# Bias and row maximum of the attention scores in one DVE operation

## The chip, the cores and the metric

The kernel runs on one core of a Trainium2 chip. The metric is the time of one execution on the device in microseconds (us), as the median of several runs. A profiled execution also gives a trace: every instruction of every engine with its start and its duration. The engines are PE (TensorE, matrix products), DVE (VectorE, elementwise work and reductions along a row), ACT (ScalarE, activation functions), POOL (GpSimd) and SP (the queue that issues the transfers). Each runs its own instructions in order and waits on semaphores for the others.

## What is computed

Two layers of a hybrid decoder over 256 tokens of width 1024. In each layer an attention group of 8 heads and a state-space group of 16 heads read the same normalised input through one input projection, and an output projection adds the result to the stream. This is the part of the reference that the change touches, cut to what matters for 256 tokens (where a query sees only the one block of its own):

```python
q = rms_norm(q.reshape(b, s, 8, 128), q_norm_w)
k = rms_norm(k.reshape(b, s, 8, 128), k_norm_w)
slopes = exp2(-8.0 * h / 8)                    # h = 1..8
s_own = einsum('hqd,hcd->hqc', q, k) * dh ** -0.5
s_own = s_own - slopes * (t_query - t_key)
s_own = where(t_query >= t_key, s_own, -inf)
p = softmax(s_own, axis=-1)
attn = einsum('hqc,hcd->hqd', p, v) * silu(g)
```

## The kernel before

Activations lie with 128 partitions; tokens come in two tiles of 128. Every projection is computed as three products of a split form (fp32r): the weights are split into a high part `wh` (an ACT cast, line 101) and a low part `wl` (a DVE subtraction, line 102), the input into `hT` and `lT`, and PE adds high x high, low x high and high x low (lines 226 to 228 with tokens on the partitions, lines 244 to 246 with channels on them). The weights, about 77 MB, stream in by DMA into four `raw` buffers; up to eight split pieces are held ahead of PE.

The projections go through in the order v, q and k of heads 0 to 3, q and k of heads 4 to 7, x (the state-space input, tiles `xb`), g, z, and the output. The small products of attention and of the state-space part are laid between them: each is a generator that yields a number of ticks and goes on that many weight pieces later. A scheduler then orders the instructions of every engine by its own estimate of when their inputs are there, so that the written order is a priority and not the final order. It stands ahead of the run: the engines follow the order that it fixed.

`qk_post` normalises q and k. ACT squares and sums a tile of 4 heads (`ss`), DVE computes `se` (line 344, 128x4: for q it is `ss + 128 eps`, so that the factor 128^-0.5 of the scores is in it), POOL raises it to the power -0.5 (`rr`, line 185), DVE multiplies (`qn`, line 348), PE transposes (`qtp`, line 354), and ACT writes `qT` or `kT`.

`attn_head` does one head. PE computes the scores `sp` of both query tiles in PSUM (line 362: the first 128 queries against 128 keys; line 363: the second 128 against 256), so a row of 384 holds 128 and then 256 scores. DVE adds the bias (line 365): `base` holds the distance and the causal mask without the slope, and one operation over 384 columns multiplies it by the slope and adds the scores. Two reductions give the negated maxima `mx` (lines 367 and 368). ACT takes the exponential with `mx` as bias and sums it (lines 370 and 371). DVE takes the reciprocal and scales both parts (lines 374 to 376). PE then transposes the probabilities (`pp`, line 380), ACT copies them (`pT`, line 382), and PE multiplies by v (`po`, lines 386 and 387). There are 8 heads a layer, 16 in all.

## Time and profile before

| | |
|---|---|
| time, median of 3 runs | 453.02 us (452.85 to 453.19) |
| the profiled execution: its time | 452.3 us |
| the profiled execution: its span | 450.5 us |
| PE busy | 446.1 us, 99% of the span |
| weight loads of PE (PEld) | 406.0 us, 90% |
| DVE busy | 346.7 us, 77% |
| ACT busy | 279.7 us, 62% |
| POOL busy | 23.9 us, 5% |
| granted clock of PE | full in all slices |

The span runs from the first to the last instruction that the profile shows; some 1.8 us of the execution's time lie around it. Busy times of one engine do not add to those of another: they overlap. A matmul's duration in the trace is longer than the step from its start to the next one's start, since matmuls are pipelined, so PE's steps are read from the starts.

### The profile page before, as it was taken

To read this page: it belongs to the slowest core of one execution; us is meant where nothing else is said; L and a number is where in the kernel's file an instruction comes from. 1 tells how busy PE (TensorE), PEld (TensorE's weight loads), DVE (VectorE), ACT (ScalarE), POOL (GpSimd) and SP (SyncE) were. 2 spreads that over 40 slices of the span, in tenths; PEclk is the share of its full clock that TensorE was granted. 3 is DMA by queue.
4 is the path that set the end of the run, shared out by engine and by line. 5 is a ranking of instruction groups with operands and counts; after the bars stand their busy time and mean duration, and the time that the engine had idled before them with its cause. 6 is when DMAs were issued, how large, how long until landed. Compare 5 with 4: busy or idle time off the path is not lost.

```text
span 450.5 us, 7880 instructions
## 1 busy us (share of the span) xinstructions
PE 446.1 (99%) x2956; PEld 406.0 (90%) x2956; DVE 346.7 (77%) x636; ACT 279.7 (62%) x571; POOL 23.9 (5%) x29
## 2 busy tenths in 40 slices
PE   9999999999999999999999999999999999999997
PEld 9998878999999999888899878889999989998986
DVE  7597876799999888766565784686999999787621
ACT  7776779778558645534556656977657865555400
POOL 0000320200000000000000011110000000000000
PEclk9999999999999999999999999999999999999999
DMA  8888886452355155556246988561435444553301
GB/s 282 275 250 294 284 302 249 143 185 95 95 188 176 60 160 186 169 188 182 61 138 232 284 278 288 185 227 53 139 109 175 139 141 128 200 180 121 121 25 70
DMA packets 26373, 79.43 MB, mean 176 GB/s; under 512 B 2624, under 2 KB 9440, under 8 KB 25824
## 3 DMA queue, kind: packets, MB, share of 16 engines
q1 hardware_dynamic: 26048, 78.68, 53.3%
q8 instruction: 23, 0.38, 0.3%
q10 hardware_dynamic: 288, 0.27, 0.2%
q14 instruction: 14, 0.11, 0.1%
HBM read 77.85 MB, written 1.08 MB: 175 GB/s over the span
## 4 chain that ended last, share of the span: by engine, by line
PE 99%; DVE 0%; issue 0%
PE o L227 6%; PE o L226 6%; PE o L228 6%; PE xb L244 5%; PE xb L246 5%; PE xb L245 5%; PE z L245 3%; PE v L228 3%; PE z L244 3%; PE v L226 3%; PE v L227 3%; PE z L246 3%; PE k L227 3%; PE g L246 3%; PE g L244 3%; PE g L245 3%
## 5 line engine op out<-in xcount | busy, mean ns | idle before, releaser
L102 DVE TENSOR_TENSOR wl<-raw,wh 128x1024 fp32r<-128x1024 f32 (+3 forms) x145 | 166.0, 1157 | 41.3 <-ACT wh L101 40.1
L101 ACT CAST wh<-raw 128x1024 fp32r<-128x1024 f32 (+3 forms) x145 | 143.9, 999 | 59.8 <-DMA raw<-in_w_dram 15.9
L244 PE MATMUL xb<-hT,wh 128*128 128x256 f32 x192 | 56.3, 293 | 0.0
L245 PE MATMUL xb<-lT,wh 128*128 128x256 f32 x192 | 54.4, 283 | 0.0
L246 PE MATMUL xb<-hT,wl 128*128 128x256 f32 x192 | 53.9, 281 | 0.0
L245 PEld LDWEIGHTS xb<-lT,wh 128*128 128x128 f32 x192 | 36.2, 189 | 0.3
L246 PEld LDWEIGHTS xb<-hT,wl 128*128 128x128 f32 x192 | 36.2, 189 | 0.1
L244 PEld LDWEIGHTS xb<-hT,wh 128*128 128x128 f32 x192 | 36.2, 188 | 0.2
L246 PE MATMUL g<-hT,wl 128*128 128x256 f32 x128 | 36.3, 283 | 0.0
L245 PE MATMUL z<-lT,wh 128*128 128x256 f32 x128 | 36.2, 283 | 0.0
L244 PE MATMUL g<-hT,wh 128*128 128x256 f32 x128 | 36.1, 282 | 0.0
L244 PE MATMUL z<-hT,wh 128*128 128x256 f32 x128 | 36.0, 281 | 0.0
L245 PE MATMUL g<-lT,wh 128*128 128x256 f32 x128 | 35.9, 281 | 0.0
L246 PE MATMUL z<-hT,wl 128*128 128x256 f32 x128 | 35.9, 280 | 0.0
L447 DVE SCALAR_TENSOR_TENSOR cv<-rw,par_sb,cv 128x256 f32<-128x256 f32 x72 | 31.6, 481 | 4.2 <-ACT cv L444 4.2
L226 PE MATMUL k<-wh,hT 128*128 128x512 f32 x64 | 25.4, 397 | 0.0
L227 PE MATMUL k<-wh,lT 128*128 128x512 f32 x64 | 25.4, 397 | 0.0
L228 PE MATMUL k<-wl,hT 128*128 128x512 f32 x64 | 25.4, 397 | 0.0
L227 PE MATMUL q<-wh,lT 128*128 128x512 f32 x64 | 25.1, 394 | 0.0
L226 PE MATMUL q<-wh,hT 128*128 128x512 f32 x64 | 25.1, 394 | 0.0
L227 PE MATMUL o<-wh,al 128*128 128x512 f32 (+1 forms) x64 | 24.7, 386 | 0.0
L228 PE MATMUL q<-wl,hT 128*128 128x512 f32 x64 | 24.6, 395 | 0.0
(197 smaller groups left out, 1106.6 us busy)
## 6 DMA issues: line engine op xcount, KB each, us to landing
raw<-in_w_dram SPq DMA_DIRECT2D x120, 512.0 KB, 4.3
raw<-in_w_dram SPq DMA_DIRECT2D x15, 348.0 KB, 3.7
cb<-cd SPq DMA_DIRECT2D x4, 1024.0 KB, 7.8
raw<-in_w_dram SPq DMA_DIRECT2D x8, 344.0 KB, 3.6
x<-in_x_dram SPq DMA_DIRECT2D x2, 512.0 KB, 5.2
xT<-in_w_dram SPq DMA_DIRECT2D x3, 256.0 KB, 4.3
out_dram<-x SPq DMA_DIRECT2D x3, 256.0 KB, 2.0
raw<-in_w_dram SPq DMA_DIRECT2D x2, 174.0 KB, 3.2
```

The source lines that it names most:

```text
L101: nc.scalar.copy(h[:, ks, :wd], src[:, ks, :wd])
L102: nc.vector.tensor_tensor(lo[:, ks, :wd], src[:, ks, :wd], h[:, ks, :wd].bitcast(F32), ALU.subtract)
L226: pe.matmul(ps[:, cs], lh[:, kl, tl], wh[:, kk, cs], start=first, stop=False)
L227: pe.matmul(ps[:, cs], ll[:, kl, tl], wh[:, kk, cs], start=False, stop=False)
L228: pe.matmul(ps[:, cs], lh[:, kl, tl], wl[:, kk, cs], start=False, stop=final)
L244: pe.matmul(o, wh[:, kk, cs], lh[:, k, :], start=(k == 0 and c == 0), stop=False)
L245: pe.matmul(o, wh[:, kk, cs], ll[:, k, :], start=False, stop=False)
L246: pe.matmul(o, wl[:, kk, cs], lh[:, k, :], start=False, stop=(k == KT - 1 and c == 1))
L447: dve.scalar_tensor_tensor(cv[:, c, :], rw[:, c, k:k + S], cw(k), cv[:, c, :], ALU.mult, ALU.add)
```

## The change

For each head the multiplication of `base` by the slope is taken out of the DVE operation. Scores and bias are held divided by the slope: q carries the factor 1/slope, put in through `slope2` (the squared slope of every head, 8 memsets on POOL at the start) in the small operation `se` of q; the exponential multiplies by the slope again through its scale. With no factor left, bias and maximum are one DVE operation (`tensor_tensor_reduce`: add, then maximum along the row), once for the 128 and once for the 256 columns. A small operation of 128x2 multiplies both maxima by minus the slope.

```diff
+    slope2 = const.tile([P, NH], F32, name="slope2")
+    for h in range(NH):
+        pool.memset(slope2[:, h:h + 1], 4.0 ** -(h + 1))
@@ qk_post
-        dve.tensor_scalar(se, ss, a, b, ALU.mult, ALU.add)
+        if col == C_QN:
+            dve.scalar_tensor_tensor(se, ss, b, slope2[:, 4 * c:4 * c + 4], ALU.add, ALU.mult)
+        else:
+            dve.tensor_scalar(se, ss, a, b, ALU.mult, ALU.add)
@@ attn_head
-        dve.scalar_tensor_tensor(sc, base, 2.0 ** -(h + 1), sp[:, 0:384], ALU.mult, ALU.add)
+        mp = small.tile([P, 2], F32, tag="mp", name="mp")
+        for i, cs in enumerate((slice(0, 128), slice(128, 384))):
+            dve.tensor_tensor_reduce(sc[:, cs], base[:, cs], sp[:, cs], 1.0, -3.0e38,
+                                     ALU.add, ALU.max, mp[:, i:i + 1])
         mx = small.tile([P, 2], F32, tag="mx", name="mx")
-        dve.tensor_reduce(mx[:, 0:1], sc[:, 0:128], AX.X, ALU.max, negate=True)
-        dve.tensor_reduce(mx[:, 1:2], sc[:, 128:384], AX.X, ALU.max, negate=True)
+        slope = 2.0 ** -(h + 1)
+        dve.tensor_scalar(mx, mp, -slope, None, ALU.mult)
-        act.activation(sc[:, 0:128], sc[:, 0:128], AF.Exp, bias=mx[:, 0:1], accum_out=sm[:, 0:1])
+        act.activation(sc[:, 0:128], sc[:, 0:128], AF.Exp, bias=mx[:, 0:1], scale=slope,
+                       accum_out=sm[:, 0:1])
```

(and the same scale in the second exponential). In the built program each of the two new operations is a pair: the operation over the row, and one of 128x1 that writes the maximum. The scheduler orders all engines anew. On DVE, at the first head of the first layer, this stands in a row before (`se` belongs to k of heads 4 to 7, `wl` is a weight piece's low part):

```order
L365 SCALAR_TENSOR_TENSOR sc<-base,sp 128x384
L344 TENSOR_SCALAR se<-ss 128x4
L102 TENSOR_TENSOR wl_973<-raw_877,wh_972 128x1024
L367 TENSOR_REDUCE mx<-sc 128x1
L368 TENSOR_REDUCE mx<-sc 128x1
L344 TENSOR_SCALAR se<-ss 128x4
```

and this now:

```order
L374 ISA sc,mp<-base,sp 128x128
L374 ISA mp 128x1
L374 ISA sc,mp<-base,sp 128x256
L374 ISA mp 128x1
L350 TENSOR_SCALAR se<-ss 128x4
L102 TENSOR_TENSOR wl_983<-raw_887,wh_982 128x1024
L378 TENSOR_SCALAR mx<-mp 128x2
L350 TENSOR_SCALAR se<-ss 128x4
```

The weight piece stands between the scores and the maximum in both; three operations of the head have become five. On PE, where that first head's probabilities are transposed (`pp`) in the stream of the x projection, this stood in a row:

```order
L244 MATMUL xb_1072<-hT_135,wh_754 128x256
L245 MATMUL xb_1072<-lT_136,wh_754 128x256
L246 MATMUL xb_1072<-hT_135,wl_755 128x256
L244 MATMUL xb_1072<-hT_135,wh_754 128x256
L245 MATMUL xb_1072<-lT_136,wh_754 128x256
L246 MATMUL xb_1072<-hT_135,wl_755 128x256
L244 MATMUL xb_1072<-hT_135,wh_772 128x256
L245 MATMUL xb_1072<-lT_136,wh_772 128x256
L380 MATMUL pp<-ident,sc 128x128
L354 MATMUL qtp<-ident,qn 128x128
L380 MATMUL pp<-ident,sc 128x128 x2
L354 MATMUL qtp<-ident,qn 128x128 x7
```

and this stands there now, from the same matmul on:

```order
L247 MATMUL xb_1083<-hT_144,wh_763 128x256
L391 MATMUL pp<-ident,sc 128x128
L360 MATMUL qtp<-ident,qn 128x128
L391 MATMUL pp<-ident,sc 128x128 x2
L360 MATMUL qtp<-ident,qn 128x128 x7
L248 MATMUL xb_1083<-lT_145,wh_763 128x256
L249 MATMUL xb_1083<-hT_144,wl_764 128x256
```

The transposes stand seven matmuls of the x projection earlier. PE's instructions are the same 2611 rows in both programs, in another order at such places; the runs of plain fp32 products that interrupt the split ones are 71 before and 76 now. The order on SP is unchanged, and up to the first head DVE's differs only in the kind of the `se` of q.

## Rows read from the trace of the kernel before

**Rows 1.** The page: span, busy time of each engine, slices of DVE and PE's clock.
```profile
span 450.5 us, 7880 instructions
...
PE 446.1 (99%) x2956; PEld 406.0 (90%) x2956; DVE 346.7 (77%) x636; ACT 279.7 (62%) x571; POOL 23.9 (5%) x29
...
DVE  7597876799999888766565784686999999787621
...
PEclk9999999999999999999999999999999999999999
```
**Rows 2.** The page's chain that ended last, shares of the span by engine.
```profile
PE 99%; DVE 0%; issue 0%
```
**Rows 3.** Waits of PE, all of them: who waited for whom, us, times, longest.
```profile
PE warm L165 <- DVE ones L159: 1.1, 1, 1.1
```
**Rows 4.** Timeline of PE: start us, us, line, operation, tiles; an alone-standing score product.
```profile
80.55 0.38 PE L362 MATMUL sp<-kT,qT 128*128 128x128 f32 x2
80.77 0.60 PE L363 MATMUL sp<-kT,qT 128*128 128x256 f32 x2
81.02 0.47 PE L244 MATMUL xb<-hT,wh 128*128 128x256 f32 x1
81.32 0.28 PE L245 MATMUL xb<-lT,wh 128*128 128x256 f32 x1
81.44 0.28 PE L246 MATMUL xb<-hT,wl 128*128 128x256 f32 x1
```
**Rows 5.** Timeline of PE: first head's transposes (pp) and what follows without a break.
```profile
86.89 0.27 PE L380 MATMUL pp<-ident,sc 128*128 128x128 f32 x1
87.00 0.27 PE L354 MATMUL qtp<-ident,qn 128*128 128x128 f32 x1
87.11 0.38 PE L380 MATMUL pp<-ident,sc 128*128 128x128 f32 x2
87.33 0.93 PE L354 MATMUL qtp<-ident,qn 128*128 128x128 f32 x7
88.09 0.39 PE L362 MATMUL sp<-kT,qT 128*128 128x128 f32 x2
88.32 0.60 PE L363 MATMUL sp<-kT,qT 128*128 128x256 f32 x2
88.56 0.47 PE L246 MATMUL xb<-hT,wl 128*128 128x256 f32 x1
88.87 0.28 PE L244 MATMUL xb<-hT,wh 128*128 128x256 f32 x1
```
**Rows 6.** Timeline of DVE: the first head's probabilities are scaled, last part.
```profile
84.03 0.35 DVE L376 TENSOR_SCALAR sc<-sc,ri 128x256 f32<-128x256 f32 x1
```
**Rows 7.** Groups by line: out<-in, shapes, xcount | busy us, mean ns | idle before.
```profile
L365 DVE SCALAR_TENSOR_TENSOR sc<-base,sp 128x384 f32<-128x384 f32 x16 | 8.8, 551 | 1.6 <-PE sp L363 0.9 <-PE pp L380 0.5
...
L368 DVE TENSOR_REDUCE mx<-sc 128x1 f32<-128x256 f32 x16 | 6.6, 411 | 0.0
...
L367 DVE TENSOR_REDUCE mx<-sc 128x1 f32<-128x128 f32 x16 | 4.5, 282 | 0.1
...
L370 ACT ACTIVATION_READ_ACCUMULATOR sc<-sc,mx 128x1 f32 x16 | 3.2, 200 | 0.0
...
L344 DVE TENSOR_SCALAR se<-ss 128x4 f32<-128x4 f32 x16 | 2.6, 162 | 0.0
...
L458 DVE SCALAR_TENSOR_TENSOR cm<-bp,tri 128x256 f32<-128x256 f32 x4 | 1.7, 414 | 0.0
...
L460 DVE SCALAR_TENSOR_TENSOR cm<-bp,tri 128x128 f32<-128x128 f32 x4 | 1.1, 282 | 0.0
...
L526 DVE TENSOR_SCALAR nv<-np 128x2 f32<-128x2 f32 x4 | 0.6, 151 | 0.0
```
**Rows 8.** Timeline of POOL: its work at the start.
```profile
0.83 0.56 POOL L169 IOTA io<- 128x512 f32 x1 [0.39 <-POOLq L754]
16.68 0.56 POOL L185 TENSOR_TENSOR rs<-me,mhalf 128x1 f32<-128x1 f32 x1 [15.28 <-DVE me L308]
```

## The prediction

> **What bounds the kernel now.** I read the page's busy times first: of a span of 450.5 us PE is busy for 446.1, DVE for 346.7, ACT for 279.7 [rows 1]. That alone does not settle it, since matmuls overlap in the trace. The second view is the chain that ended last, followed back from the last instruction: 99% of it is PE, and DVE has 0% [rows 2]. The third is the list of PE's waits, and it holds one line: 1.1 us ahead of the warm-up matmuls at the very start [rows 3]. So no score, mask or probability keeps PE waiting long enough to be listed. The fourth is the timeline of PE, for which the starts count: two split matmuls of 256 columns stand 0.12 us apart (81.32 and 81.44), and the next product starts at that pace whatever it belongs to [rows 4]. [...] The kernel is a stream of matmuls that PE takes one after the other, and its time is the sum of their steps.

> DVE matters only where it is late for PE. It is 90% busy or more in slices 9 to 13 and 29 to 34 [rows 1], some 90 to 146 and 315 to 383 us, and the heads lie in and just ahead of these stretches. There the question is how much time passes between the end of DVE's work for a head and PE's use of it. For the first head the last scaling of the probabilities ends at 84.03 + 0.35 = 84.38 [rows 6], and the two transposes that need it start at 87.11 [rows 5]: a margin of 2.7 us.

> **The change part by part, DVE.** A head loses one operation of 551 ns and two reductions of 411 and 282: 1244 ns [rows 7]. It gains two combined operations, two writes of the maximum and one of 128x2. The trace has no combined operation. Its nearest rows are the two-input operations that also read PSUM: 282 ns for 128 columns and 414 for 256 [rows 7], 696 together; that is the lower end, as the maximum comes on top of it. The upper end is that the row is passed twice, once to add and once to reduce: 282 + 282 and 414 + 411, 1389 together [rows 7]. I take the lower, because the new instruction reads the same two inputs and writes the same output as those rows. The write of the maximum has no row on DVE; the nearest is ACT's read of its accumulator, 200 ns, and on the low side it could hide wholly behind the next operation, 0; the smallest DVE operation shown, of 128x2, takes 151 [rows 7], and I take that for it and for the product with the slope. The sum is 696 + 3 x 151 = 1149 ns, 0.1 us less a head, 1.5 us over 16 heads. The ends are 696 + 0 + 151 = 847 and 1389 + 400 + 151 = 1940, so 0.4 us less to 0.7 us more a head.

> [...]

> None of this is on the path that sets the end: what covers it is PE's own stream, and DVE's 1.5 us stay as idle time of DVE. If the cover went (PE waiting for a head), each us that a head comes late would count in full.

> **The small edits.** The `se` of q becomes an operation of the same size with one more input, 162 ns before [rows 7], eight times; anything up to twice that, 0.16 us, lies ahead of a POOL operation and a transpose, and only the q tiles wait for it. I put it at nothing, with 0.2 us for the range. The scale in the exponential is an operand of an operation that is there already: nothing. The eight memsets of `slope2` stand on POOL behind the iota, which ends at 0.83 + 0.56 = 1.39 us, and POOL's next work begins at 16.68 [rows 8]; at the iota's 0.56 us each, the dearest row, they would take 4.5 us of the 15 that are idle there. Nothing. The first exponential of a head now waits for both maxima instead of its own: 0.41 us later than before at most [rows 7], out of the margin.

> **PE's order.** PE's instructions are the same, so its sum of steps can change only through neighbours. The runs of plain fp32 products among the split ones go from 71 to 76, which looks like five more interruptions. Their price is read from two places. The score products alone, from 80.55 to the second split matmul after them at 81.32, less one step of 0.12, cost 0.65 us [rows 4]. Behind eleven transposes the same products, from 88.09 to 88.87 less 0.12, cost 0.66 [rows 5]. Breaking a run up costs 0.01 us, so five breaks cost nothing that can be seen; I allow 0.3 us either way.

> The order also spends margin. The first head's transposes stand seven split matmuls earlier, 7 x 0.12 = 0.8 us, so they come at 87.11 - 0.8 = 86.3, and 1.9 of the 2.7 us are left. Against that stand 0.1 us gained on DVE (0.7 lost at the upper end) and 0.4 for the later first exponential. It remains positive at both ends: 1.6 and 0.8 us.

> **The sum.** Against the profiled execution, 450.5 of span and 1.8 around it: PE's steps 0 (within 0.3), DVE 0 on the path, `se` 0 to 0.2, start 0. That gives 452.3 for an execution like the profiled one. The three runs have their median at 453.02, 0.7 higher, so the forecast for the median is 453.0.

> **Rivals.** *Slower: the combined operation is much dearer than its parts, and PE waits for the heads.* The point from which this decides is a head that ends more than the 1.9 us later than before; or a lasting excess, since where DVE is full [rows 1] a head's excess is handed to the next. At the upper end of 0.7 us a head, 8 heads a layer would gather 5.6 us if DVE had no idle time at all between them; less 1.9 of margin that is 3.7 a layer, 7.4 for both, 460.4. With half of the excess caught by DVE's idle time it is 2.8 - 1.9 = 0.9 a layer, 454.8. For it: no row shows the operation, and DVE is full in those slices. Against it: the excess needs the upper end of every bound at once. I give it 0.09.

> *Faster: PE has room that its busy time hides, and DVE's saving comes out.* Then up to 16 x 0.4 = 6.4 us at the lower end of DVE's cost, or 1.5 at my value, would show: 446.6 or 451.5. For it is that PE's busy time counts overlapping matmuls, and that weight loads fill only 406.0 us [rows 1]. Against it are the chain, the single wait, and starts that follow each other at a constant step [rows 2 to 5]: nothing there waits for DVE. I give it 0.04. [...]

> *The change does not do what it says:* if the combined operation passes the row twice, DVE does not become faster at all. That alone leaves the time at 453.0, since only the slow rival's excess is felt; it is in the first case.

> **How the numbers follow.** What a measurement of this kernel can tell from no change is about 0.2%, 0.9 us. The forecast, no change, has 0.87; the slow rival 0.09; the fast one 0.04. These are also the chances of same, slower and faster. For the range I take the spread of the runs and PE's 0.3 below, which gives 452.4, and above the 0.3 of PE, 0.2 of `se`, the spread, and some tenths of waiting, 454.1. That leaves out most of both rivals, less than 2 in 10.

> **What would show it.** In the profile of the changed kernel PE's list of waits should again hold the warm-up alone, the chain should stay at 99% PE, and the span should lie within half a us of 450.5. DVE's busy time should fall by 1 to 3 us; the combined rows should take about 282 and 414 ns. The forecast is wrong if a transpose of probabilities or a score product appears among PE's waits, if the weight pieces on DVE come late in slices 9 to 13 or 29 to 34, or if PE's steps at the 76 interruptions turn out longer than the same contents before.

## The result and the profile after

The changed kernel takes 456.69 us (median of 4 runs, 456.24 to 457.53); the kernel before, timed beside it, takes 452.94 (452.70 to 453.19). The ratio is 1.0084, with a 95% interval of 1.0063 to 1.0104. The forecast was 453.0 and no change: it was 3.7 us too low, and 456.69 lies above its range of 452.4 to 454.1. The kernel before ran again beside every experiment below, and one of those runs, at 1574.94 us, is left out of all ratios.

The profiled execution of after took 457.53 us, the highest of the four, with a span of 455.6; before it was 450.5 [rows 1]. So 5.1 us of span are to be found. First the page of after: span, busy times, PE's clock in 40 slices, and the chain that ended last.

```profile
span 455.6 us, 7918 instructions
...
PE 450.7 (99%) x2956; PEld 407.2 (89%) x2956; DVE 342.3 (75%) x668; ACT 280.7 (62%) x571; POOL 27.2 (6%) x37
...
PEclk9999999999999999999999999999999999999999
...
PE 85%; DMA 6%; DVE 3%; ACT 3%; issue 2%; POOL 0%; SPq 0%; ACTq 0%; POOLq 0%
```

DVE's busy time fell by 4.4 us, from 346.7. PE's rose by 4.6, from 446.1, with the same 2956 instructions and the clock granted in full in every slice, as in [rows 1]. The second view is PE's list of waits (us in total, times, longest).

```profile
PE warm L165 <- DVE ones L159: 1.1, 1, 1.1
PE pp L391 <- DVE sc L386: 0.4, 1, 0.4
PE v L231 <- DVE wl L102: 0.2, 1, 0.2
```

Two waits are new against [rows 3], 0.6 us together. They don't make 5.1, though the chain seems to say more, with PE at 85% where [rows 2] had 99%. Its list in order of time shows why: at PE's wait for the scaled probabilities (`sc`), at 88.28 us, the chain, followed back, leaves PE, and it has no piece of PE's from there down to 22.5 us. Three of its pieces (start, us, what):

```profile
31.10 4.40 DMA raw<-in_w_dram
...
66.27 10.44 DMA raw<-in_w_dram
...
85.92 0.69 DVE qn L354
```

In all that time PE was working. A wait of 0.4 us is enough for the other path to be the one that ended last; the shares don't say what it cost. The rest has to lie between PE's instructions, so the third view is PE's timeline, read by its starts. Here are two ends of the same stretch of the k projection, 20 steps of 512 columns apart with nothing between them. Before:

```profile
41.34 0.39 PE L226 MATMUL k<-wh,hT 128*128 128x512 f32 x1
...
45.91 0.39 PE L228 MATMUL k<-wl,hT 128*128 128x512 f32 x1
```

After:

```profile
42.26 0.39 PE L229 MATMUL k<-wh,hT 128*128 128x512 f32 x1
...
46.92 0.39 PE L231 MATMUL k<-wl,hT 128*128 128x512 f32 x1
```

That is 4.57 / 20 = 0.2285 us a step before and 4.66 / 20 = 0.233 after. **Each matmul starts later behind the last one, though nothing waits and the clock is full.** The durations (0.39) don't show it; only the starts do. In the x projection, where a step has 256 columns, 26 steps lie between these rows of before:

```profile
82.01 0.28 PE L245 MATMUL xb<-lT,wh 128*128 128x256 f32 x1
...
84.96 0.28 PE L244 MATMUL xb<-hT,wh 128*128 128x256 f32 x1
```

and between these of after:

```profile
82.93 0.28 PE L249 MATMUL xb<-hT,wl 128*128 128x256 f32 x1
...
86.00 0.28 PE L248 MATMUL xb<-lT,wh 128*128 128x256 f32 x1
```

2.95 / 26 = 0.1135 before, 3.07 / 26 = 0.118 after. The slow pace is not new in itself. In the z projection the kernel before has it too: 32 steps of its timeline, from 161.38 to 165.15, take 0.118 each.

```profile
161.38 0.28 PE L246 MATMUL z<-hT,wl 128*128 128x256 f32 x1
...
165.15 0.28 PE L245 MATMUL z<-lT,wh 128*128 128x256 f32 x1
```

So before has two paces, in 512 columns as well: 20 steps of q, from 250.82 to 255.49, take 0.2335 each. After has the quick one of 256 columns in places (10 steps of x, from 321.56 to 322.69, take 0.113 each) and the slow one more of the time. Of neighbouring split matmuls of 256 columns, some 490 pairs start 0.11 us apart in before's timeline and some 355 in after's; of 512 columns, some 95 pairs start 0.22 apart in before's and none in after's. To put one number on it, I took from each trace all pairs of neighbouring split matmuls of the same width with nothing between them (about 680 pairs of 512 columns, 1330 of 256) and the mean distance of their starts: 229.9 and 116.4 ns before, 233.3 and 117.4 after. The program has 720 matmuls of 512 and 1440 of 256: 720 x 3.4 = 2.5 us and 1440 x 1.0 = 1.4, together **3.9 of the 5.1 us**. The first head's wait gives 0.4. Some 0.6 pass at the very start: the v projection's matmul behind the second new wait starts at 25.83, its counterpart before at 25.25. That leaves 0.2; the 288 matmuls of 344 and 348 columns in the v projections are not in this count.

The medians differ by 3.75 us, less than the spans of the two profiled executions. The pace alone is enough for that.

### The profile page after: what moved, and what is told of

The parts are those of the page before. It is cut to its first block, busy times and chain, and to the rows that moved or that the text cites. A ratio compares the mean times of both kernels' runs of the same rounds, so it can differ in the third digit from the quotient of the medians.

```text
span 455.6 us, 7918 instructions
## 1 busy us (share of the span) xinstructions
PE 450.7 (99%) x2956; PEld 407.2 (89%) x2956; DVE 342.3 (75%) x668; ACT 280.7 (62%) x571; POOL 27.2 (6%) x37
## 4 chain that ended last, share of the span: by engine, by line
PE 85%; DMA 6%; DVE 3%; ACT 3%; issue 2%; POOL 0%; SPq 0%; ACTq 0%; POOLq 0%
PE o L229 6%; PE o L231 6%; PE o L230 6%; DMA raw<-in_w_dram 5%; PE xb L249 4%; PE xb L248 4%; PE xb L247 4%; PE g L247 3%; PE z L248 3%; PE g L249 3%; PE z L247 3%; PE g L248 3%; PE z L249 3%; PE v L231 3%; PE v L229 3%; PE v L230 3%
## 5 line engine op out<-in xcount | busy, mean ns | idle before, releaser
L188 POOL TENSOR_TENSOR rr<-se,mhalf 128x4 f32<-128x4 f32 x16 | 19.1, 1192 | 121.3 <-DVE se L348 82.3
L229 PE MATMUL o<-wh,ah 128*128 128x512 f32 (+1 forms) x64 | 24.7, 386 | 0.0
```

Source lines behind the costliest of these rows:

```text
L188: pool.tensor_tensor(o, i, mhalf[:, :n], ALU.pow)
L229: pe.matmul(ps[:, cs], lh[:, kl, tl], wh[:, kk, cs], start=first, stop=False)
```

## The experiments

What could change the step of an unchanged matmul? The change adds two tiles to SBUF. `slope2`, 32 bytes per partition, stands in the first pool, ahead of all operands of the projections. `mp`, four buffers of 32 bytes, stands in the pool of small tiles, which lies between the activations (`hT`, `lT`) and the weight buffers (`raw`, `wh`, `wl`). In the built program the first `hT` lies at byte 38016 of a partition before and 38048 after, the first `wh` at 162752 and 162912. All activations have moved by 32 bytes, all weights by 160, and the distance between the two operands of a split matmul has grown by 128. The theories were: operands have to lie at multiples of 64 bytes; the address of one operand decides; the distance between the two decides; the heads' new work costs the time after all. In every kernel below the order of PE's, ACT's and DVE's instructions is that of its parent; a kernel made from before has one or two memsets more on POOL.

**Alignment.** After, with `slope2` twice as large, so that all operands are at multiples of 64 again.

```diff
-    slope2 = const.tile([P, NH], F32, name="slope2")
+    slope2 = const.tile([P, 2 * NH], F32, name="slope2")
```

> The changed kernel with slope2 made 64 instead of 32 bytes wide per partition (half of it unused), so that every tile behind it starts 32 bytes later and on a multiple of 64 again; the order of every engine is that of the changed kernel. Theory A (the addresses: the 32 bytes of slope2 shift the matmul operands and the DMA targets off multiples of 64, and PE's steps become longer: 512 columns 233 instead of 229 ns, 256 columns 118 instead of 114): the slow steps become as rare as in the kernel before, time 452.5 to 453.9. Theory B (the combined operation and the new order make PE wait): nothing changes, 456.2 to 457.5. Theory C (the price of 4 us is spread over both): 454 to 455.5.

Measured: 457.17 us, 1.0093 of before (1.0078 to 1.0108), steps of 233.3 and 117.6 ns. Nothing came back. The distance is still 128 larger: alignment to 64 is not the cause. The time is also what was expected if the combined operation and the new order made PE wait; that theory falls with the whole change at the old distance, below.

**Moving all, the activations, or the weights of the kernel before.** Three kernels without any part of the change. The first puts an unused tile of 32 bytes into the first pool (everything moves by 32), the second one there and one in the small pool (activations by 32, weights by 64), the third only one in the small pool (weights by 32).

```diff
+    gap = const.tile([P, 8], F32, name="gap")
+    pool.memset(gap, 0.0)
+    gap2 = small.tile([P, 8], F32, tag="gap2", name="gap2", bufs=1)
+    pool.memset(gap2, 0.0)
```

> The kernel before with an unused 32-byte tile ahead of the big tiles (one memset on POOL more), so that these start 32 bytes later; the order of every engine is that of the kernel before. Theory A: slow steps nearly everywhere, time 455.5 to 457. Theory B: no change, 452.7 to 453.3. Theory C: 454 to 455.5.

> The kernel before with two unused 32-byte tiles: one ahead of all big tiles, one behind the activations and ahead of the weight buffers. The activations (hT, lT, qT, kT, x) start at 32 of 64 bytes, raw, wh and wl at 0. Theory A with the activations as the cause: 455.5 to 457. Theory A with the weight buffers as the cause: 452.5 to 453.5. Theory B: 452.7 to 453.3.

> The kernel before with one unused 32-byte tile behind the activations: raw, wh and wl start at 32 of 64 bytes, the activations at 0. Theory A with the weight buffers as the cause: 455.5 to 457, and the first weight pieces land later than 3.7 us. Theory A with the activations as the cause: 452.5 to 453.5. Theory B: 452.7 to 453.3.

Measured: everything moved 451.98 us, 0.998 (0.997 to 0.9991); activations and weights by different amounts 457.70, 1.0126 (1.0089 to 1.0163); weights alone 458.31, 1.0119 (1.0095 to 1.0144). The first and the third have `wh` at the same address and differ by 6 us; the first and the second have `hT` at the same address and differ by as much. Neither address decides alone. **An unused tile of 32 bytes between the two costs the kernel before at least as much as the whole change does** (1.0119 against 1.0084; the intervals overlap from 1.0095 to 1.0104). The timeline of PE of the third kernel, the same 20 steps of k:

```profile
41.90 0.40 PE L228 MATMUL k<-wh,hT 128*128 128x512 f32 x1
...
46.57 0.39 PE L230 MATMUL k<-wl,hT 128*128 128x512 f32 x1
```

4.67 / 20 = 0.2335 us a step, as after.

One rival is left here: the tiles on which DVE and ACT work lie ahead of the weights as well, so their distance has changed too, and the other engines might disturb PE's reads. Near the end of the kernel they do next to nothing. These are two stretches of 5 us, of the kernel before and then of the one with its weights moved (busy us of PE, PEld, DVE, ACT and POOL with their instructions, PE's clock, the share of DMA, GB/s), and under each PE's rows 15 steps apart in it:

```profile
430.00:435.00 5.00, 5.00 (x26) 4.17 (x25) 0.27 (x1) 0.00 (x0) 0.00 (x0) 1.00 0.02 3
...
431.10 0.39 PE L226 MATMUL o<-wh,sh 128*128 128x512 f32 x1
...
434.53 0.39 PE L226 MATMUL o<-wh,sh 128*128 128x512 f32 x1
```

```profile
435.00:440.00 5.00, 5.00 (x24) 4.08 (x23) 0.45 (x1) 0.00 (x0) 0.00 (x0) 1.00 0.02 3
...
435.15 0.40 PE L228 MATMUL o<-wh,sh 128*128 128x512 f32 x1
...
438.65 0.39 PE L228 MATMUL o<-wh,sh 128*128 128x512 f32 x1
```

3.43 / 15 = 0.2287 against 3.50 / 15 = 0.2333 us a step, with ACT idle and DVE busy for 0.27 and 0.45 of the 5 us. The slow pace does not need the other engines.

None of the three lies in a range that was expected for it. The first should have been slow if alignment decided, and came out below even the range for no effect; the other two were 0.7 and 1.3 us slower than the slowest expected.

**The whole change at the old distance.** After, with `mp` in a pool of its own ahead of the activations. The weights then lie exactly where they lie in after, at 162912, and the activations have moved up behind `mp`, to 38176.

```diff
+    mpool = ctx.enter_context(tc.tile_pool(name="mpool", bufs=4))
...
-        mp = small.tile([P, 2], F32, tag="mp", name="mp")
+        mp = mpool.tile([P, 2], F32, tag="mp", name="mp")
```

> The changed kernel, instruction for instruction, with the four buffers of mp taken out of the pool between the activations and the weight buffers and laid ahead of both. The weight buffers keep the changed kernel's addresses; the activations start 128 bytes later, so that the distance from hT to wh is that of the kernel before (124736 bytes). Theory D (the distance between activations and weight buffers sets PE's step): the quick steps come back and the time is 451.5 to 453.9, with whatever the heads cost, 0 to 0.8 us, on top of that of the shifted kernel before, 451.98. Theory B (the combined operation and the order make PE wait): 456 to 457.5, as the changed kernel.

Measured: 452.73 us, 1.0006 of before (0.9989 to 1.0024); steps of 229.3 and 115.9 ns. Every operation of the change is in it, and the loss is gone. Its page and PE's waits:

```profile
span 450.2 us, 7918 instructions
...
PE 445.5 (99%) x2956; PEld 405.6 (90%) x2956; DVE 341.6 (76%) x668; ACT 280.5 (62%) x571; POOL 29.1 (6%) x37
...
PE 98%; DVE 1%; POOL 0%; issue 0%; POOLq 0%
```

```profile
PE pp L392 <- DVE sc L387: 0.3, 1, 0.3
```

DVE has its 4 to 5 us less work, PE is back at 445.5, and the first head still keeps PE waiting for 0.3 us (more on that below).

**How much distance.** The kernel before, with an unused tile of 64 to 256 bytes between activations and weights (16 to 64 columns in place of 32 here):

```diff
+    gap2 = small.tile([P, 32], F32, tag="gap2", name="gap2", bufs=1)
+    pool.memset(gap2, 0.0)
```

> The kernel before with one unused tile of 128 bytes between the activations and the weight buffers, the shift that mp makes in the changed kernel; the order of every engine is that of the kernel before, the scores are computed as before. Theory D: slow steps nearly everywhere, 455.5 to 458.5. Theory B: 452.7 to 453.3.

> The kernel before with an unused tile of 256 bytes between the activations and the weight buffers. Theory D with a period of 256 bytes or less above 128: as the kernel before, 452.5 to 453.5; with any change of the distance harmful, 455.5 to 458.5. Theory B: 452.7 to 453.3.

> The kernel before with an unused tile of 64 bytes between the activations and the weight buffers. Theory D with a period of 64 bytes: as the kernel before, 452.5 to 453.5 (the 128 bytes of the run before would then do nothing either); otherwise 455.5 to 458.5. Theory B: 452.7 to 453.3.

> The kernel before with 96 unused bytes between the activations and the weight buffers. Theory D, the distance counted modulo 256 bytes, with the old distance alone quick: 455.5 to 458.5. Theory D with a band of quick distances that begins below 128 (where 455.46 was measured, less than at 32 and 64): 453.5 to 456. Were the distance without effect: 452.3 to 453.3.

> As the run at 96, with 160 unused bytes. Old distance alone quick: 455.5 to 458.5. A band of quick distances from 160 on: 451 to 453.5, at or below the kernel before. Without effect: 452.3 to 453.3.

> As the run at 96, with 192 unused bytes: distance a multiple of 256. Old distance alone quick: 455.5 to 458.5. A band of quick distances: 449 to 453, below the kernel before if the middle of the band is the best place. Without effect: 452.3 to 453.3.

> As the run at 96, with 224 unused bytes, 32 short of the period of 256. Old distance alone quick: 455.5 to 458.5. A band of quick distances: 449 to 453. Without effect: 452.3 to 453.3.

Measured, with the kernels of 0 and 32 bytes above beside them (the mean steps as explained above; each ratio is to the kernel before that ran beside it):

| bytes added between | time, us | ratio to before (95%) | step of 512, ns | step of 256, ns |
|---|---|---|---|---|
| 0 (before) | 452.94 | 1 | 229.9 | 116.4 |
| 32 (weights alone) | 458.31 | 1.0119 (1.0095 to 1.0144) | 233.5 | 118.0 |
| 64 | 457.65 | 1.0107 (1.0087 to 1.0127) | 232.3 | 118.7 |
| 96 | 460.30 | 1.0160 (1.0131 to 1.0190) | 234.2 | 119.8 |
| 128 | 455.46 | 1.0062 (1.0047 to 1.0077) | 233.3 | 116.8 |
| 160 | 455.94 | 1.0074 (1.0038 to 1.0111) | 233.1 | 117.1 |
| 192 | 456.10 | 1.0074 (1.0044 to 1.0103) | 227.6 | 119.7 |
| 224 | 457.79 | 1.0105 (1.0073 to 1.0136) | 233.3 | 118.2 |
| 256 | 453.12 | 0.9996 (0.9978 to 1.0014) | 229.9 | 116.4 |

At 256 bytes the kernel before is back, steps and all; at 128 it is not. The eight distances within 256 differ by up to 1.6%, and the one that the kernel before happened to have is the quickest of them. 96 bytes cost more than any expectation had. With 128 bytes and none of the change, 2.7 us of the loss are there (455.46 against 452.76 beside it). The other 1.0 us of the 3.75 was not taken apart: after's steps of 256 columns, with the activations 32 bytes further on, are 0.6 ns longer than this kernel's, an estimated 0.9 us over 1440 of them.

The row of 192 is odd: 512 columns go faster there than anywhere else, 256 columns slower than nearly everywhere. Its timeline of PE, 20 steps across q and k and 32 steps of x:

```profile
41.28 0.39 PE L228 MATMUL q<-wh,hT 128*128 128x512 f32 x1
...
45.81 0.39 PE L230 MATMUL k<-wl,hT 128*128 128x512 f32 x1
...
81.75 0.28 PE L247 MATMUL xb<-lT,wh 128*128 128x256 f32 x1
...
85.58 0.28 PE L246 MATMUL xb<-hT,wh 128*128 128x256 f32 x1
```

4.53 / 20 = 0.2265 and 3.83 / 32 = 0.120. What PE loads ahead of a matmul is 128x128 in both kinds, as PEld's timeline of before shows:

```profile
41.11 0.19 PEld L226 LDWEIGHTS k<-wh,hT 128*128 128x128 f32 x1
...
81.21 0.19 PEld L245 LDWEIGHTS xb<-lT,wh 128*128 128x128 f32 x1
```

In the program the 128x128 operand is the activations in the first kind, with 512 columns of weights as the other one; in the second it is the weights, with 256 columns of activations. In the table 512 columns are quickest at 192 (227.6) and 256 columns at 0 and 256 (116.4), and the time counts their sum: 456.10 at 192, 452.94 at 0. Which of their two differences matters, the operand that is loaded or the number of columns, is open: the output projection has 256-column matmuls of the first kind, and 19 steps of them take 0.120 in this trace as well (424.74 to 427.02).

**The change at addresses that the kernel before had, too.** After with the pool of `mp` behind all others, so that `hT` and `wh` lie at the same bytes as in the kernel before moved by 32. That kernel was run again beside it, on the same chip. A third kernel moves the weight operands `wh` and `wl` by 32 bytes and leaves the landing buffers `raw` of the DMA and the activations where they were.

```diff
+    gpool = ctx.enter_context(tc.tile_pool(name="gpool", bufs=1))
...
+    gap2 = gpool.tile([P, 8], F32, tag="gap2", name="gap2")
+    pool.memset(gap2, 0.0)
```

> The changed kernel, instruction for instruction, with mp laid behind the weight buffers: activations and weight buffers have exactly the addresses of the shifted kernel before (32 bytes later than in the kernel before), so that the heads' own cost is what is left between this run and that one. Heads cost nothing: 451.5 to 452.4, as the shifted kernel. Heads cost the wait seen at the first head: 452.4 to 453.2. Theory B: 456 or more.

> The kernel before with an unused 32-byte tile ahead of all big tiles, once more and beside the run above on the same chip. Theory D: quick steps as in the kernel before, 451.5 to 453.3; if its small lead over the kernel before was the chip, the ratio is 1.000 within 0.001, otherwise 0.998.

> The kernel before with an unused 32-byte tile between the raw buffers and wh: the DMA's targets (raw) and the activations keep their addresses, only the weight operands of the matmuls (wh and wl) start 32 bytes later. The matmul operands' distance as the cause: 455.5 to 458.5, slow steps. The raw buffers (DMA, the engines' reads of them) as the cause: 452.3 to 453.5.

Measured: the change at these addresses 452.43 us (12 runs), 0.9988 of before (0.9976 to 0.9999); the kernel before moved by 32 bytes 452.20 (11 runs), 0.9982 (0.9969 to 0.9995); weight operands alone moved 458.19, 1.0110 (1.0086 to 1.0134). Three things follow. The last kernel shows that it is the operands of PE and not where the DMA lands. The first two differ by 0.2 us, and their intervals overlap for the most part: with the addresses held, **no cost or gain of the change itself can be told from none** (452.43 lies on the line that its expectation drew between the two). And both are 0.1 to 0.2% faster than the kernel before, and the steps of 256 columns fit that: they take 115.7 to 115.9 ns in all four traces of the old distance whose activations have moved, and 116.4 in the two where they have not (before, and with 256 bytes between). The change at the old distance is one of the four, and its time, 1.0006 (0.9989 to 1.0024), does not show the gain. The two have the lowest ratios of all versions.

## The first head's wait

[rows 6] and the transposes of [rows 5] had a margin of 2.7 us, of which 0.8 to 1.6 should have been left. After has none left: PE waits for 0.36. The timeline of PE in after:

```profile
87.64 0.28 PE L247 MATMUL xb<-hT,wh 128*128 128x256 f32 x1
88.28 0.33 PE L391 MATMUL pp<-ident,sc 128*128 128x128 f32 x1 [0.36 <-DVE sc L386]
```

Followed backwards, DVE's timeline has the last scaling at 88.14 (before 84.03), behind a `qn` of k that itself waits for POOL:

```profile
80.88 2.36 DVE L102 TENSOR_TENSOR wl<-raw,wh 128x1024 fp32r<-128x1024 f32 x2 [0.67 <-ACT wh L101]
83.16 0.28 DVE L374 CUSTOM_DVE_ANT_0 sc<-base,sp 128x128 f32<-128x128 f32 x1
...
85.92 0.69 DVE L354 TENSOR_TENSOR qn<-k,rr 128x512 f32<-128x512 f32 x1 [0.75 <-POOL rr L188]
...
87.75 0.16 DVE L385 RECIPROCAL ri<-sm 128x2 f32<-128x2 f32 x1
87.94 0.29 DVE L386 TENSOR_SCALAR sc<-sc,ri 128x128 f32<-128x128 f32 x1
88.14 0.35 DVE L387 TENSOR_SCALAR sc<-sc,ri 128x256 f32<-128x256 f32 x1
```

But the head is late before that: its first operation starts at 83.16, behind two weight pieces (`wl`) that wait for ACT's casts. PE's score product of that head started at 79.32, so DVE left it lying for over 3 us. Before, the product started at 77.83 and DVE's first operation on it at 78.83. ACT's timeline tells why the casts are late (`ehi` is a decay of the state-space part, `cb` a transfer of 1 MB):

```profile
73.00 2.45 ACT L481 ACTIVATE ehi<-cb,nac 128x128 f32<-128x128 f32 x8 [3.03 <-DMA cb<-cd]
```

The casts stand behind `ehi` on ACT, and `ehi` waits 3.0 us for the landing of `cb`. At this place the kernel before doesn't wait for it at all:

```profile
68.66 2.46 ACT L470 ACTIVATE ehi<-cb,nac 128x128 f32<-128x128 f32 x8
```

`cb` comes in two transfers, and `ehi` starts when the first has landed. That one takes the shorter time in each of these lines, of before and then of after:

```profile
DMA to landing us min/median/max: 4.1/5.9/7.7
...
DMA to landing us min/median/max: 7.6/8.6/9.7
```

Issued at 64.4 and at 65.4, it is there at 68.6 and at 72.9. In the change at the addresses of the kernel before moved by 32 bytes the same wait is shorter:

```profile
71.39 2.46 ACT L482 ACTIVATE ehi<-cb,nac 128x128 f32<-128x128 f32 x8 [1.79 <-DMA cb<-cd]
```

and there the head is in time again: the scaling's last row and the second transposes, which need it, from the timelines of DVE and PE:

```profile
86.53 0.35 DVE L388 TENSOR_SCALAR sc<-sc,ri 128x256 f32<-128x256 f32 x1
```

```profile
87.28 0.38 PE L392 MATMUL pp<-ident,sc 128*128 128x128 f32 x2
```

86.88 against 87.28, a margin of 0.4. So four traces of the same order give 3.0, 2.6, 1.8 and 1.6 us of ACT's wait and 0.36, 0.3, 0 and 0 of PE's (the second is the change at the old distance, the last the kernel of the alignment experiment). Why `cb` lands at different times was not tried; each case is one trace, with the weight transfers running beside it.

## Why the prediction was wrong, point by point

**DVE's part was right in kind, and its smallest term was too dear.** These are the groups of after by line (busy us, mean ns of one):

```profile
L374 DVE CUSTOM_DVE_ANT_0 sc<-base,sp 128x256 f32<-128x256 f32 x16 | 6.7, 417 | 0.0
...
L374 DVE DVE_READ_ACCUMULATOR2_ANT mp<- 128x1 f32 x32 | 2.7, 83 | 0.0
L378 DVE TENSOR_SCALAR mx<-mp 128x2 f32<-128x2 f32 x16 | 2.6, 165 | 0.1
...
L348 DVE SCALAR_TENSOR_TENSOR se<-ss,slope 128x4 f32<-128x4 f32 x8 | 1.2, 155 | 0.0
```

The combined operation takes 417 ns for 256 columns and 283 for 128, as its nearest rows said (414 and 282 [rows 7]): the 411 and 282 that the upper end had for a second pass are not in it. The term that was mis-sized is the write of the maximum: 83 ns, forecast 151. It adds hardly anything to DVE's time, since it starts together with the operation behind it, as here at the first head:

```profile
83.36 0.08 DVE L374 DVE_READ_ACCUMULATOR2_ANT mp<- 128x1 f32 x1
83.36 0.42 DVE L374 CUSTOM_DVE_ANT_0 sc<-base,sp 128x256 f32<-128x256 f32 x1
```

That is the low side that the prediction named and did not take. By durations a head takes 417 + 283 + 2 x 83 + 165 = 1031 ns in place of 1244, against 1149 forecast: 16 x 0.21 = 3.4 us less, forecast 1.5. The busy time, which counts overlaps once, fell by 4.4 where 1 to 3 were expected. None of it is on the path, as the prediction had it: the change at the old distance has the same saving and the time of before.

**The small edits were right.** The `se` of q takes 155 ns (162 before), the exponential 410 and 505 ns with the slope as scale (411 and 508 before), and neither POOL nor ACT appears among PE's waits.

**The step that failed is "PE's steps 0 (within 0.3)" in the sum, and under it the sentence that PE's sum of steps "can change only through neighbours".** This step took the instructions as the whole description of PE's work: same instructions, same interruptions, so the same time. The operands' addresses were left out, though the diff shows two new tiles and one of them lies, with its four buffers, between the operands of every split matmul. Measured, the term is about 3.9 us of the profiled span. A sign was there to be read: the pace of 0.1135 and that of 0.118 both stand in the trace of before. The reading of [rows 4] and the margin's arithmetic used 0.12 for both. Nor does the next product start at that pace "whatever it belongs to": behind the score products a split matmul starts 0.30 us ahead of the next one (81.02 and 81.32 [rows 4]).

**PE's order: the price of interruptions is not what failed, the margin is.** With the addresses held, the new order and all else in the change came to 0.2 us more than the kernel before, within the noise. The step "It remains positive at both ends: 1.6 and 0.8 us" was wrong, and no bound there contained it. It counted what the head's own operations and PE's order do to the margin, and not the wait that stands two engines back: ACT's for `cb`, ahead of the casts, ahead of the weight pieces, ahead of the head on DVE. It cost 0 to 0.4 us, and alone it would have left the forecast of no change standing.

**The rivals.** The slow one had the right sign and the wrong cause: the combined operation is at the low end of its cost, and DVE is less busy. The fast one, that DVE's saving would come out, fell: with PE's pace restored, DVE's 341.6 us in place of 346.7 bring nothing (1.0006). That the change doesn't do what it says fell with the 417 ns.

**The chances.** The 0.2% as what can be told from no change was an estimate that no row had shown; the result's interval, 1.0063 to 1.0104, is 0.2% to each side. 0.09 for slower stood for one mechanism. The change's new tiles brought another, 2.7 us with the 128 bytes alone, which no step of the sum named.

## What to carry to other kernels

Here PE was the bound, and an unused tile of 32 bytes between the operands, without a matmul more, took the kernel to 458.31 us, 1.0119 of before. So where a change adds, removes or resizes a tile, compare the addresses of the matmul operands in the two built programs, above all the distance between the two operands of a matmul, before comparing work. Before a slowdown is put down to a new operation, run the new kernel with its tiles placed so that the operands lie as before, and the old one with an unused tile of the same size. And read PE's pace as the distance of starts over many steps: at 0.01 us a row, 229 and 233 ns can't be told apart in one step, while 20 steps show it.

## What was not expected of the hardware

Three things stay open. Why the distance matters: no run shows a mechanism. Why a kernel, at one distance, has both paces in different stretches: the output projection's steps of 256 columns are even shorter after (0.1135 us each from 448.00 to 449.93) than before (0.118 from 442.77 to 446.89). And why activations that lie 32 bytes or more further on, at the same distance, change a step of 256 columns by some 0.6 ns: 115.7 to 115.9 against 116.4 at the old distance, and 117.4 (after) against 116.8 with 128 bytes more.
